# A hybrid decoder step whose first layer reads feature-major tokens and applies the norm to the sums

## The chip, the cores and the metric

The kernel runs on one core of a Trainium2 chip. The metric is device time in microseconds (us). The engines are PE (TensorE, matmuls and weight loads), DVE (VectorE), ACT (ScalarE), POOL (GpSimd) and SP (SyncE, which here issues nearly all DMAs). Each engine works through its own list of instructions in order, and semaphores tie the lists together.

## The reference

Two layers of a decoder run over 512 prompt tokens and 32 sample tokens of 1024 features. Cut to what matters:

```python
def _rmsnorm(x, w):
    return x * lax.rsqrt(jnp.mean(x * x, axis=-1, keepdims=True) + EPS) * w

h = _rmsnorm(x, norm_w)
z = h @ w_in                      # 1024 x 3584, split into ten parts
rq, rk, rv, rg, mq, mk, mv, mg, pu, pg = jnp.split(z, _split_points(), axis=-1)
# rq rk rv rg: retention; mq mk mv mg: block-sparse attention; pu pg: pooling
mq = _rope(_rmsnorm(_heads(mq), q_norm_w), pos)
mix = concat([r_o * silu(rg), m_o * silu(mg), p_o * silu(pg)])
y = x + mix @ w_out
```

Since 1/rms is one number per token, `h @ w_in` equals `((x * w) @ w_in) * (1/rms)`: the factor may be put on the sums.

## The kernel before

All matmuls of the projections are in fp32r with a split into a high and a low part: tokens and weights each become a rounded part and a remainder, and three products (high by high, low by high, high by low) are summed in PSUM. The split tokens lie in `XT`, feature-major (128 features in the partitions, 8 k-tiles, 544 tokens). The weights of a projection ("chunk") come in four slices of two k-tiles; `load_weights` issues their DMAs, `split_weights` has ACT write the high part into `whl` and DVE or POOL subtract for the low part. There are five `whl` buffers, four of which one chunk takes.

In layer 0 the tokens arrive token-major: `start` and `start2` load four tiles of 128 tokens, `rmsnorm` squares them on ACT, POOL takes the root, DVE multiplies by 1/rms and by the norm weights (spread over the partitions by two small matmuls in `spread_row`), PE transposes eight 128 x 128 blocks a tile, and ACT and DVE write the high and the low part into `XT`. Layer 1 does the same with the output of layer 0.

Then `dense` runs the chunks in the order mv, mq, mk, pu, pg, mg, rq, rv, rk, rg, o0, o1, o2. `tok_piece` takes a tile of 128 tokens against 384 (or 256) columns, 8 k-tiles by three products, 24 matmuls into one of two `acc` banks; `feat_piece` (pu and the gates) puts features in the partitions and 256 or 288 tokens in the columns. Sample tokens go through `sample_piece` into the bank `dec`, straight from the raw weights. After each piece a "post" task reads the bank: a copy (mv, rv), squares, rope and norm (`projected`: mq, mk), or tanh and two multiplications (`post_gate`).

The order on each engine is written out by a planner (`_Plan`). Tasks are generators that yield the engine wanted, the flags waited for and the buffers needed; the planner picks whichever can start first by its own table of costs, and for tasks that allow two engines (`ACT|DVE`, `DVE|POOL`, `ACT|POOL`) also the engine. What it picks is then fixed, and at run time every engine follows its list.

Of the kernel before, what the change touches and what calls it, by code (L numbers as in the profile page):

```python
# [18 lines left out]
D = 1024  # L19
# [273 lines left out]
def trunk(ctx, tc, depth, xp, xs, kv, sret, spool, pt, nrow, lpar, w384, w256, cst, y0,  # L293
# [93 lines left out]
    klz = const.tile([128, H, SEQ], F32R, name="klz")  # L387
    Sst = [const.tile([128, 3, 128], F32, name=f"Sst{i}") for i in range(2)]
# [17 lines left out]
    def raw_tag(ci, s_):  # L406
        return "pk" if ci == 0 and s_ > 1 else "wraw"
# [113 lines left out]
    def rmsnorm(l, t, L):  # L521
# [3 lines left out]
        if t == 4:  # L525
            yield R("SP", [("ys", l)], ["P", "P"])
            x = [buf("P")[:rows] for _ in range(2)]
            for half in range(2):
                S.dma_start(x[half], (xs if l == 0 else y0[SEQ:, :])[:, half * 512:half * 512 + 512])
                X.flag("xs", l, at=X.dma(64))  # L530
# [7 lines left out]
        else:  # L538
            x = ytile(t)
            first = l == 0 and t == 0  # L540
            pair = "xn", t // 2
            yield R("ACT", [("y", 0, 0, 0) if first else ("y", l, t)] + [("xn", l, t)] * (t % 2),
                    [] if t % 2 else [tag])
# [5 lines left out]
            if first:  # L549
                A.activation(xn3[:, 0:4], x[:, 0:4], AF.Square, accum_out=st[:, 0:1])  # L550
                yield R("ACT", [("y", 0, 0, 1)])
                A.activation(xn3[:, 4:8], x[:, 4:8], AF.Square, accum_out=st[:, 1:2])
                yield R("POOL")
                G.tensor_tensor(out=st[:, 0:1], in0=st[:, 0:1], in1=st[:, 1:2], op=OP.add)
            else:
                A.activation(xn3, x, AF.Square, accum_out=st[:, 0:1])
                yield R("POOL")
# [38 lines left out]
    def join_sample(a, out, W):  # L596

        half = W // 2
        yield R("ACT", (), ["t2"])
        t_ = buf("t2")  # L600
        A.copy(t_[:64, :half], a[64:128, :half])
        yield R("DVE")
        for m in range(2):
            rows = slice(NS * m, NS * m + NS)
            V.tensor_tensor(out=out[:, m * half:(m + 1) * half], in0=a[rows, :half], in1=t_[rows, :half], op=OP.add)
        X.put("t2")
        X.put("dec")

    def projected(a, dst, t, Ct, St, scale=None):
# [25 lines left out]
        if scale is None:  # L635
# [5 lines left out]
            rsq(st[:rows, 1, :H], st[:rows, 0, :H], H, rows, 1.0 / HD)  # L641
# [129 lines left out]
    def layer(l):  # L771
# [3 lines left out]
        def parameters():  # L775
            yield R("SP", (), ["pt"])
# [7 lines left out]
            else:  # L784
                S.dma_start(rowp[0:1, :D], nrow[l:l + 1, :D])
                X.flag("row1", at=X.dma(4))
                X.spawn(spread_row(), 0)
            X.flag("rowp issued", l)
            yield R("SP", [("cst1 issued",)])
# [4 lines left out]
            yield R("DVE", [("normed", l)])  # L794
            X.put("pt")

        def spread_row():

            yield R("POOL")
            ones = L["rowp"][0:1, D + 256:D + 384]  # L800
            G.memset(ones, 1.0)
            L["row"] = []
            for i, tag in enumerate(("pv", "dec")):
                yield R("PE", [("row1",)], [tag])
                a = ps(tag)
                mm(a, ones, L["rowp"][0:1, i * 512:(i + 1) * 512])
                L["row"].append(a)
                X.flag("row", l, i)
            X.spawn(warm(WARM), 0)
            yield R("DVE", [("normed", l)])  # L810
            X.put("pv")
            X.put("dec")
# [155 lines left out]
        def post_mq(t):  # L968
            def f(a):
                yield R("DVE", [("tabs", l, 0)], ["qk"])  # L970
                q_ = buf("qk")
                yield from projected(a, q_, t, L["tabs", 0][:, 0, t], L["tabs", 0][:, 1, t])
# [24 lines left out]

        def post_mv(t):
            def f(a):
                if t == 0:  # L1000
                    yield R("DVE", (), ["tv"])
                    L["tv"] = buf("tv").rearrange("p (t n) -> p t n", t=4)
                if t < 4:
                    yield R("ACT|DVE")
                    copy(L["tv"][:, t], a[:, :384])
                    X.put("acc")
                    X.flag("tv", l, t)
                    send(o_vp[l, t * 128:(t + 1) * 128], L["tv"][:, t], 196)
# [12 lines left out]
        def post_mk(t):  # L1021
            def f(a):
# [4 lines left out]
                yield from projected(a, k_, t, L["tabs", 1][:, 0, t], L["tabs", 1][:, 1, t])  # L1027
# [173 lines left out]
        def post_gate(k, half, sample_first, keys, done):  # L1201
# [4 lines left out]
            def f(a):  # L1206
                yield R("ACT", (), ["t1"])
# [17 lines left out]
        def post_rq(t):  # L1225
            def f(a):
# [3 lines left out]
                yield from projected(a, q_, t, cos[:, t], sin[:, t], False if t < 4 else rqs[:rows, t])  # L1230
# [13 lines left out]
        def post_rv(t):  # L1244
            def f(a):
# [3 lines left out]
                if t < 4:  # L1249
                    yield R("ACT|DVE")  # L1250
                    copy(L["rtv"][:, t], a[:, :384])
                    X.put("acc")
                    X.flag("rtv", l, t)
                else:
                    yield R("ACT", (), ["ks"])
                    vs = L["rvs"] = buf("ks")
                    yield from join_sample(a, vs[:NS], 384)
# [7 lines left out]
        def post_rk(t):  # L1265
            def f(a):
# [6 lines left out]
                yield from projected(a, k_, t, cos[:, t], sin[:, t], rks[:rows, t])  # L1273
# [54 lines left out]
        def ret_chunk(c):  # L1328
# [30 lines left out]
            yield from group_norm(on, H, reps[:, c])  # L1359
# [157 lines left out]
        def dense():  # L1517
# [7 lines left out]
            seen4 = [("x", l, 4, 0), ("x", l, 4, 1)]  # L1525
# [8 lines left out]
            yield from tokens("mv", post_mv, lambda t: [("x", l, t, 0), ("x", l, t, 1)])  # L1534
# [189 lines left out]
```

## Time and profile before

| | us |
|---|---|
| median of 3 runs | 717.33 |
| lowest, highest run | 715.79, 717.79 |
| the profiled execution | 717.02 |
| its span, first to last instruction | 715.3 |
| PE busy | 688.0 |
| DVE busy | 478.4 |
| ACT busy | 331.1 |
| POOL busy | 142.7 |

The span is 1.7 us shorter than the time of the same execution. Busy times are sums over the whole program and say little of a stage; for the stage that the change touches, the first 40 us, the rows further down give times from the span's start.

### The profile page before, as it was taken

What the parts mean: (1) busy time and instruction counts of PE and PEld (TensorE: products, weight loads), DVE (VectorE), ACT (ScalarE), POOL (GpSimd) and SP (SyncE); (2) the same over time, 40 slices, a digit from 0 to 9 for tenths busy, and PEclk for the clock granted to TensorE, in tenths of its full rate; (3) what the DMA queues carried; (4) which work ended last, traced back from release to release, by engine and by line L of the source; (5) the groups of instructions that cost most, each with busy time, mean ns of one, the idle gap of its engine ahead of it and who ended that gap; (6) DMA issues with size and microseconds to landing.
All of it is one profiled execution on the core that took longest, in us unless ns stands there. A gap on an engine that the chain in (4) does not pass through costs nothing.

```text
span 715.3 us, 16993 instructions
## 1 busy us (share of the span) xinstructions
PE 688.0 (96%) x5960; PEld 574.5 (80%) x5960; DVE 478.4 (67%) x1096; ACT 331.1 (46%) x844; POOL 142.7 (20%) x171
## 2 busy tenths in 40 slices
PE   7999989999999997989999999999999999999898
PEld 4888767777878796979989777777777878889798
DVE  4567888867554559786475688986845555887632
ACT  5535557663423413375164246776624234247511
POOL 5122422301001004342050223330101010035100
PEclk9999989999999999999999999999999999999999
DMA  9848888989999875005655679999999995020452
GB/s 282 262 129 254 283 259 277 291 272 315 303 329 309 255 286 167 21 2 185 216 149 173 199 257 324 286 309 298 293 298 322 316 317 178 23 76 2 161 179 77
DMA packets 113177, 159.76 MB, mean 223 GB/s; under 512 B 13763, under 2 KB 97860, under 8 KB 113093
## 3 DMA queue, kind: packets, MB, share of 16 engines
q1 hardware_dynamic: 112564, 158.43, 68.8%
q8 instruction: 47, 0.77, 0.4%
q14 instruction: 38, 0.30, 0.1%
q10 hardware_dynamic: 528, 0.26, 0.1%
HBM read 148.80 MB, written 9.84 MB: 222 GB/s over the span
## 4 chain that ended last, share of the span: by engine, by line
PE 83%; DVE 12%; issue 2%; ACT 2%; POOL 1%; DMA 1%; SPq 0%; DVEq 0%; POOLq 0%; ACTq 0%
PE acc L325 52%; PE dec L325 11%; PE pv L325 10%; PE tr L335 6%; PE att L325 3%; DVE t L287 2%; DVE whl L287 1%; DVE qk L287 1%; DVE mix L287 1%; DVE XT L287 1%; DMA pk<-kv 1%; DVE dP L287 1%; DVE P L287 1%; DVE kT L287 0%; DVE pv L287 0%
## 5 line engine op out<-in xcount | busy, mean ns | idle before, releaser
L325 PE MATMUL acc<-whl,XT 128*128 128x384 f32 (+1 forms) x1728 | 318.6, 337 | 2.4 <-DVE whl L287 1.7
L325 PEld LDWEIGHTS acc<-whl,XT 128*128 128x128 f32 x1728 | 287.6, 188 | 18.9 <-issue 13.1
L325 PE MATMUL acc<-XT,whl 128*128 128x256 f32 (+1 forms) x960 | 142.2, 299 | 1.1 <-DVE t L287 1.1
L325 PEld LDWEIGHTS acc<-XT,whl 128*128 128x128 f32 x960 | 127.3, 193 | 10.2 <-issue 8.1
L287 ACT CAST whl<-wraw 128x768 fp32r<-128x768 f32 (+1 forms) x102 | 79.1, 784 | 47.1 <-PE acc L325 32.3
L287 DVE TENSOR_TENSOR whl<-wraw,whl 128x768 fp32r<-128x768 f32 (+1 forms) x78 | 72.0, 931 | 33.5 <-ACT whl L287 31.9
L287 POOL TENSOR_TENSOR whl<-wraw,whl 128x768 fp32r<-128x768 f32 (+1 forms) x24 | 41.5, 1734 | 121.7 <-ACT whl L287 121.6
L325 PE MATMUL dec<-pk,qblk 128*32 128x256 f32 x768 | 50.9, 386 | 0.9 <-DMA pk<-kv 0.8
L325 PEld LDWEIGHTS dec<-pk,qblk 128*32 128x32 f32 x768 | 23.3, 110 | 19.7 <-issue 4.6
L287 DVE TENSOR_TENSOR pv<-pv,cst 128x384 f32<-128x384 f32 x40 | 22.5, 563 | 16.7 <-PE pv L325 16.5
L287 ACT ACTIVATE P<-att,ast 128x128 f32<-128x128 f32 (+3 forms) x48 | 25.2, 529 | 14.1 <-DVE ast L287 12.7
L287 DVE TENSOR_TENSOR mix<-acc,qk 128x384 f32<-128x384 f32 (+1 forms) x24 | 12.2, 509 | 24.9 <-PE acc L325 24.8
L287 POOL TENSOR_TENSOR qst<-qst,mhalf 128x6 f32<-128x6 f32 (+1 forms) x20 | 26.5, 1323 | 1.7
L287 POOL TENSOR_TENSOR mix<-mix,t 128x256 f32<-128x256 f32 x8 | 6.3, 789 | 102.6 <-DVE t L287 74.7
L287 ACT ACTIVATE dP<-dec,stat 128x256 f32<-128x256 f32 x32 | 15.2, 474 | 24.2 <-DVE stat L287 24.1
L287 DVE TENSOR_TENSOR t<-acc,cst 128x192 f32<-128x192 f32 (+1 forms) x48 | 17.3, 415 | 13.1 <-PE acc L325 13.1
L287 POOL TENSOR_SCALAR qst<-qst 128x6 f32<-128x6 f32 (+1 forms) x20 | 4.6, 230 | 102.1 <-DVE qst L287 98.9
L287 ACT ACTIVATE t<-acc 128x256 f32<-128x256 f32 (+1 forms) x32 | 12.6, 393 | 26.3 <-PE acc L325 24.4
L335 PE MATMUL tr<-cst,qk 128*128 128x128 f32 (+1 forms) x108 | 17.8, 273 | 4.3 <-DVE qk L287 3.8
L287 ACT COPY t<-dec 64x192 f32<-64x192 f32 (+1 forms) x18 | 5.6, 310 | 35.0 <-PE dec L325 34.8
L287 DVE TENSOR_REDUCE stat<-dec 128x1 f32<-128x256 f32 x32 | 13.5, 421 | 11.8 <-PE dec L325 11.4
L287 ACT ACTIVATE dPT<-dec 128x256 f32<-128x256 f32 x32 | 12.2, 381 | 19.6 <-PE pv L325 19.6
(469 smaller groups left out, 1210.3 us busy)
## 6 DMA issues: line engine op xcount, KB each, us to landing
pk<-kv SPq DMA_DIRECT2D x256, 192.0 KB, 3.8
wraw<-w SPq DMA_DIRECT2D x78, 384.0 KB, 4.7
wraw<-w SPq DMA_DIRECT2D x24, 256.0 KB, 4.4
y<-mix SPq DMA_DIRECT2D x4, 512.0 KB, 3.7
mix<-xp SPq DMA_DIRECT2D x3, 512.0 KB, 7.8
o_vp<-tv SPq DMA_DIRECT2D x8, 192.0 KB, 3.3
o_kp<-qk SPq DMA_DIRECT2D x8, 192.0 KB, 4.1
pt<-sret SPq DMA_DIRECT2D x2, 768.0 KB, 6.8
```

What stands on the lines that cost most here:

```text
L287: return f(*args, **kw)
L325: nc.tensor.matmul(out, lhsT, rhs, start=start, stop=stop)
L335: nc.tensor.transpose(out, in_, ident[:n, :n])
```

## The change

In layer 0 the tokens are now given in a feature-major layout (`xt`, two halves of 256 tokens by four pairs of k-tiles; `xst` for the samples), so nothing is transposed. `split_tokens` multiplies by the norm weights of the feature (`ncol`, one number per partition) while it splits: ACT or DVE writes the high part, DVE the low part. `norm_tokens` squares the tokens (`ACT|POOL`), adds the eight k-tiles (`DVE|POOL`), and a matmul with ones sums over the partitions; DVE and POOL make 1/rms per token, `rs`. `spread_norms` puts 1/rms of all tokens along the columns of `Rb` by matmuls of ones with a diagonal. The sums are then corrected: copies of mv and rv carry the scale (`scaled_copy`), the norms of mq and mk take a changed epsilon, pu and the gates are multiplied by `Rb` on DVE. The first chunk, mv, runs by k-tile pairs on two token tiles at once, first tokens 0 to 255 into the two `acc` banks, then 256 to 511 into the two `att` banks. Its raw weights lie in four `pk` buffers (two before), which the cached pages use later. Layer 1 is unchanged. The diff, cut to its core:

```diff
 def raw_tag(ci, s_):
-    return "pk" if ci == 0 and s_ > 1 else "wraw"
+    return "wraw" if ci else "pk"
...
+        def scaled_copy(out, a, t, keys=()):
+            if l:
+                yield R("ACT|DVE", keys)
+                copy(out(), a)
+                return
+            yield R("ACT|DVE", [("rs", t // 2), *keys])
+            if X.engine == "ACT":
+                A.activation(out(), a, AF.Copy, scale=rs[:, 1, t:t + 1])
+            else:
+                V.tensor_scalar(out(), a, rs[:, 1, t:t + 1], None, op0=OP.mult)
...
         def post_pu(f, half):
...
+                    yield R("DVE", [("U", l), ("Rb",)])
+                    V.tensor_tensor(out=L["U"][:, f, PBUF + n0:PBUF + n0 + 256], in0=a[:, :256],
+                                    in1=Rb[:, n0:n0 + 256], op=OP.mult)
...
         def post_gate(k, half, sample_first, keys, done):
...
+                if l == 0:
+                    yield R("DVE", [("Rb",)])
+                    V.tensor_tensor(out=a[:, :n], in0=a[:, :n], in1=Rb[:, n0:n1], op=OP.mult)
                 yield R("ACT", (), ["t1"])
                 th = buf("t1")
                 A.activation(th[:, :n], a[:, :n], AF.Tanh, scale=0.5)
...
-            yield from tokens("mv", post_mv, lambda t: [("x", l, t, 0), ("x", l, t, 1)])
+            if l:
+                yield from tokens("mv", post_mv, lambda t: [("x", l, t, 0), ("x", l, t, 1)])
+            else:
+                for h in range(2):
+                    for kp in range(4):
+                        yield R("PE", [("w", ci, kp), ("xk", h, kp)], [] if kp else ["att" if h else "acc"] * 2)
...
+                        for j in range(2):
+                            for k in (2 * kp, 2 * kp + 1):
+                                tok_piece(ci, "mv", 2 * h + j, a[j], KS_IN, k)
+                        if h:
+                            X.put("whl")
...
+    def split_tokens(h, kp):
+        cs = slice(256 * h, 256 * h + 256)
+        ks = (2 * kp, 2 * kp + 1)
+        yield R("ACT|DVE", [("xt", h, kp), ("ncol",)])
+        for k in ks:
+            if X.engine == "ACT":
+                A.activation(XT[:, k, 0, cs], mix[:, k, cs], AF.Copy, scale=ncolt[:, k:k + 1])
+            else:
+                V.tensor_scalar(XT[:, k, 0, cs], mix[:, k, cs], ncolt[:, k:k + 1], None, op0=OP.mult)
+        yield R("DVE")
+        for k in ks:
+            V.scalar_tensor_tensor(XT[:, k, 1, cs], mix[:, k, cs], ncolt[:, k:k + 1], XT[:, k, 0, cs].bitcast(F32),
+                                   op0=OP.mult, op1=OP.subtract)
+        X.flag("xk", h, kp)
+
+    def norm_tokens(h):
+        cs = slice(256 * h, 256 * h + 256)
+        tag = ("qT", "kT")[h]
+        for i in range(2):
+            yield R("ACT|POOL", [("xt", h, 2 * i), ("xt", h, 2 * i + 1)], [] if i else [tag])
...
+            if X.engine == "ACT":
+                A.activation(sq[:, 4 * i:4 * i + 4], x, AF.Square)
+            else:
+                G.tensor_tensor(out=sq[:, 4 * i:4 * i + 4], in0=x, in1=x, op=OP.mult)
+        yield R("DVE|POOL")
+        add2(sq[:, 0:4], sq[:, 0:4], sq[:, 4:8], OP.add)
+        yield R("DVE|POOL")
+        add2(sq[:, 0:2], sq[:, 0:2], sq[:, 2:4], OP.add)
+        yield R("DVE|POOL")
+        add2(sq[:, 0], sq[:, 0], sq[:, 1], OP.add)
+        yield R("PE", [("zeros",)], ["tr"])
+        p = ps("tr")
+        for j in range(2):
+            mm(p[:, j:j + 1], sq[:, 0, 128 * j:128 * j + 128], ones[:, 0:1])
...
+    def spread_norms():
...
+        for t in range(4):
+            A.mul(d_[:, t], ident, rs[:, 1, t:t + 1])
+        A.mul(ssum[:NS], ident[:NS, :NS], rs[:NS, 1, 4:5])
+        yield R("PE", (), ["tr", "tr"])
+        p, p4 = ps("tr"), ps("tr")
+        for t in range(4):
+            mm(p[:, t * 128:(t + 1) * 128], ones, d_[:, t])
+        X.put("P")
+        mm(p4[:, :NS], ones[:NS], ssum[:NS])
```

The program begins as follows on PE before the change. `tr<-cst,qT`, `tr<-cst,kT` are the transposes of prompt tokens, `acc<-whl,XT` the matmuls of mv, `pv<-pt` and `dec<-pt` the spreading of the norm weights, `att<-qblk` a matmul on zeros whose result nobody reads.

```order
L325 MATMUL att<-qblk 128x384
L325 MATMUL pv<-pt 128x512
L325 MATMUL dec<-pt 128x512
L325 MATMUL att<-qblk 128x384
L335 MATMUL tr<-cst,qT 128x128 x8
L325 MATMUL acc<-whl,XT 128x384 x18
L335 MATMUL tr<-cst,qT 128x128 x4
L325 MATMUL acc<-whl,XT 128x384 x6
L335 MATMUL tr<-cst,qT 128x128 x4
L335 MATMUL tr<-cst,kT 128x128 x4
L325 MATMUL acc<-whl,XT 128x384 x6
L335 MATMUL tr<-cst,kT 128x128 x4
```

After the change PE begins as follows; `tr<-ones,..` are the sums over the partitions, `tr<-P,ones` is the spreading of 1/rms, `dec<-wraw,X_71` is the sample piece of mq and `dec<-pk,X_71` that of mv.

```order
L325 MATMUL att<-qblk 128x384
L325 MATMUL acc<-whl,XT 128x384 x48
L325 MATMUL att<-whl,XT 128x384 x24
L325 MATMUL tr<-ones,qT 128x1 x2
L325 MATMUL att<-whl,XT 128x384 x12
L325 MATMUL tr<-ones,ssum 32x1 x4
L325 MATMUL tr<-ones,kT 128x1 x2
L325 MATMUL att<-whl,XT 128x384 x12
L325 MATMUL dec<-wraw,X_71 32x192 x16
L325 MATMUL acc<-whl,XT 128x384 x6
L325 MATMUL tr<-P,ones 128x128 x4
L325 MATMUL tr<-ssum,ones 128x32
```

The transposes are gone, the matmuls of mv stand at the head, and the small sums stand between its last pairs of k-tiles.

On POOL, behind the clearing of `klz` at the start, there stood before the roots of the first tile's norm and one low part of the weights:

```order
L287 MEMSET klz 64x3x512 x2
L287 MEMSET pt 1x128
L287 ISA
L287 TENSOR_TENSOR rst<-rst 128x1
L287 TENSOR_SCALAR rst<-rst 128x1
L287 TENSOR_TENSOR rst<-rst,mhalf 128x1
L287 TENSOR_TENSOR whl<-wraw,whl 128x768
```

Now there stand the squares of the first 256 tokens (`qT<-mix`), two of their additions (`qT<-qT`), and then the low part of mq's first slice:

```order
L287 MEMSET klz 64x3x512 x2
L287 ISA
L287 TENSOR_TENSOR qT<-mix 128x1024 x2
L287 TENSOR_TENSOR qT<-qT 128x1024
L287 TENSOR_TENSOR qT<-qT 128x512
L287 TENSOR_TENSOR whl<-wraw,whl 128x768
```

Four wide instructions have come to POOL that were not there. At the same time DVE, which began with the norm and the low parts of the first transposed tile, now has the low parts of the tokens (`XT<-mix,ncol,XT`) and all four low parts of mv's weights (`whl<-pk,whl`):

```order
L287 SCALAR_TENSOR_TENSOR XT<-mix,ncol,XT 128x256 x2
L287 TENSOR_TENSOR whl<-pk,whl 128x768 x2
L287 SCALAR_TENSOR_TENSOR XT<-mix,ncol,XT 128x256 x4
L287 TENSOR_TENSOR whl<-pk,whl 128x768 x2
L287 SCALAR_TENSOR_TENSOR XT<-mix,ncol,XT 128x256 x2
L287 TENSOR_SCALAR XT<-mix,ncol 128x256 x2
L287 SCALAR_TENSOR_TENSOR XT<-mix,ncol,XT 128x256 x8
L287 TENSOR_TENSOR X_71<-Rb,ncol 128x256
L287 TENSOR_TENSOR qT<-qT 128x256
```

Every one of the first nine wide steps reads two tensors from SBUF; before, the token steps read one of theirs from PSUM (the transposed block or the spread norm weights).

## Rows read from the trace of the kernel before

**Rows 1.** The page: busy time, share of the span and instructions.
```profile
PE 688.0 (96%) x5960; PEld 574.5 (80%) x5960; DVE 478.4 (67%) x1096; ACT 331.1 (46%) x844; POOL 142.7 (20%) x171
```

**Rows 2.** The page: the chain of waits that ended last, share by engine.
```profile
PE 83%; DVE 12%; issue 2%; ACT 2%; POOL 1%; DMA 1%; SPq 0%; DVEq 0%; POOLq 0%; ACTq 0%
```

**Rows 3.** PE in order of time: start, us, instructions, idle before and its releaser.
```profile
5.26 2.07 PE L325 MATMUL pv<-pt 1*128 1x512 f32 x2 [2.10 <-POOL pt L287]
...
12.15 0.44 PE L325 MATMUL acc<-whl,XT 128*128 128x384 f32 x1
12.87 3.24 PE L325 MATMUL acc<-whl,XT 128*128 128x384 f32 x17 [0.28 <-DVE XT L287]
...
30.33 7.65 PE L325 MATMUL acc<-whl,XT 128*128 128x384 f32 x42
37.91 1.51 PE L325 MATMUL dec<-wraw,X 128*32 128x192 f32 x32
39.35 8.68 PE L325 MATMUL acc<-whl,XT 128*128 128x384 f32 x48
...
115.86 1.02 PE L325 MATMUL dec<-tabs,par 128*128 128x512 f32 x2
```

**Rows 4.** Groups on PE, 0 to 38 us: busy, mean ns, idle before.
```profile
L325 PE MATMUL acc<-whl,XT 128*128 128x384 f32 x96 | 18.7, 345 | 0.3 <-DVE XT L287 0.3
...
L335 PE MATMUL tr<-cst,qT 128*128 128x128 f32 x16 | 3.0, 335 | 0.8 <-DVE qT L287 0.8
L335 PE MATMUL tr<-cst,kT 128*128 128x128 f32 x16 | 2.6, 283 | 1.1 <-DVE XT L287 1.1
```

**Rows 5.** SP's queue and ACT in order of time, from the start.
```profile
2.14 0.93 SPq L423 DMA_DIRECT2D wraw<-w  x2
...
3.44 0.63 ACT L287 ACTIVATE qT<-mix 128x512 f32<-128x512 f32 x1 [0.98 <-DMA mix<-xp]
...
6.37 0.83 ACT L287 CAST whl<-wraw 128x768 fp32r<-128x768 f32 x1 [1.34 <-DMA wraw<-w]
```

**Rows 6.** Stretches: PE, PEld, DVE, ACT, POOL busy, PEclk, DMA share, GB/s.
```profile
2.00:4.00 2.00, 1.17 (x2) 0.02 (x1) 0.00 (x0) 1.02 (x3) 1.89 (x3) 1.00 1.14 299
4.00:6.00 2.00, 0.74 (x1) 0.50 (x2) 0.00 (x0) 0.88 (x4) 1.77 (x5) 1.00 0.89 260
6.00:8.00 2.00, 2.00 (x4) 0.66 (x2) 0.44 (x1) 1.21 (x2) 1.12 (x2) 1.00 1.01 356
```

**Rows 7.** Groups on POOL, whole span.
```profile
L287 POOL TENSOR_TENSOR whl<-wraw,whl 128x768 fp32r<-128x768 f32 x19 | 34.9, 1837 | 115.8 <-ACT whl L287 115.8
...
L287 POOL TENSOR_TENSOR whl<-wraw,whl 128x512 fp32r<-128x512 f32 x5 | 6.7, 1342 | 5.9 <-ACT whl L287 5.7 <-DMA pk<-kv 0.2
```

**Rows 8.** Groups on DVE, whole span.
```profile
L287 DVE TENSOR_TENSOR att<-att,cst 128x256 f32<-128x256 f32 x24 | 10.2, 427 | 5.6 <-PE att L325 5.5
...
L287 DVE TENSOR_TENSOR whl<-pk,whl 128x768 fp32r<-128x768 f32 x2 | 1.9, 958 | 0.7 <-ACT whl L287 0.7
```

**Rows 9.** DVE in order of time, three places.
```profile
45.98 0.55 DVE L287 TENSOR_TENSOR qk<-t,qst 32x384 f32<-32x384 f32 x1
...
68.47 0.89 DVE L287 SCALAR_TENSOR_TENSOR tabs<-cst,pt 128x320 f32<-128x320 f32 x2
...
89.35 1.43 DVE L287 TENSOR_TENSOR ks<-t,qst 32x384 f32<-32x384 f32 x1
```

**Rows 10.** POOL in order of time, around the last of these.
```profile
87.55 2.82 POOL L287 TENSOR_TENSOR whl<-wraw,whl 128x512 fp32r<-128x512 f32 x2
```

**Rows 11.** Stretches, columns as in rows 6.
```profile
89.00:90.00 1.00, 0.00 (x0) 0.00 (x0) 0.90 (x2) 0.55 (x2) 1.00 (x1) 1.00 1.00 318
90.00:91.00 1.00, 0.07 (x1) 0.10 (x2) 0.97 (x2) 0.00 (x0) 0.37 (x1) 0.67 0.76 263
...
96.00:97.00 1.00, 1.00 (x13) 0.45 (x16) 0.37 (x2) 0.51 (x2) 0.00 (x0) 0.50 0.95 272
```

**Rows 12.** A group on PE, whole span: pieces of gates and pu, 256 tokens.
```profile
L325 PE MATMUL acc<-XT,whl 128*128 128x256 f32 x480 | 70.5, 297 | 0.7 <-DVE t L287 0.7
```

More of the change, by code (lines that the diff above doesn't have):

```diff
@@ L548, in rmsnorm @@
             xn3 = col3(xn)
[L549 to L557, printed above, removed]
+            A.activation(xn3, x, AF.Square, accum_out=st[:, 0:1])
+            yield R("POOL")
             x, xn = [x[:, 0:4], x[:, 4:8]], [xn[:, 0:512], xn[:, 512:D]]
@@ L793, in parameters @@
             yield from tables(1)
-            yield R("DVE", [("normed", l)])
+            yield R("DVE", [("normed", l)] if l else ())
             X.put("pt")
[L797 to L812, printed above, removed]
         def scales():
@@ L1002, in f @@
                     L["tv"] = buf("tv").rearrange("p (t n) -> p t n", t=4)
+                    X.flag("tvb", l)
                 if t < 4:
-                    yield R("ACT|DVE")
-                    copy(L["tv"][:, t], a[:, :384])
-                    X.put("acc")
+                    yield from scaled_copy(lambda: L["tv"][:, t], a[:, :384], t, [("tvb", l)])
+                    X.put("acc" if l or t < 2 else "att")
                     X.flag("tv", l, t)
@@ L1249, in f @@
                 if t < 4:
-                    yield R("ACT|DVE")
-                    copy(L["rtv"][:, t], a[:, :384])
+                    yield from scaled_copy(lambda: L["rtv"][:, t], a[:, :384], t)
                     X.put("acc")
@@ L1572, in begin @@
             X.spawn(scales(), 6)
[L1573 to L1574 removed]
+            if l:
+                for t in range(5):
+                    X.spawn(rmsnorm(l, t, L), 0)
         return {"dense": dense, "begin": begin, "L": L}
     def start():
[L1579 to L1584 removed]
@@ new lines, in split_sample @@
+    def split_sample():
+        x3 = Rb[:, :8 * NS].rearrange("p (k n) -> p k n", k=8)
+        cs = slice(SEQ, NTOK)
+        yield R("DVE", [("xst",), ("ncol",)])
+        V.tensor_tensor(out=X32, in0=x3, in1=ncolt[:, :, None].to_broadcast([128, 8, NS]), op=OP.mult)
+        yield R("ACT")
+        A.copy(XT[:, :, 0, cs], X32)
+        q3 = Rb[:, 8 * NS:16 * NS].rearrange("p (k n) -> p k n", k=8)
+        A.activation(q3, x3, AF.Square)
+        yield R("DVE")
+        V.tensor_tensor(out=XT[:, :, 1, cs], in0=X32, in1=XT[:, :, 0, cs].bitcast(F32), op=OP.subtract)
+        V.tensor_reduce(out=ssum, in_=q3.rearrange("p k n -> p n k"), axis=AX, op=OP.add)
+        X.flag("x", 0, 4, 0)
+        X.flag("x", 0, 4, 1)
+        yield R("PE", [("zeros",)], ["tr"], COLS32)
+        p = ps("tr")
+        for j in range(4):
+            mm(p[32 * j:32 * j + 32, 0:1], ssum, ones[:, 0:1])
+        yield R("DVE")
+        V.tensor_scalar(rs[:, 0, 4:5], p[:, 0:1], 1.0 / D, EPS, op0=OP.mult, op1=OP.add)
+        X.put("tr")
+        yield R("POOL")
+        G.tensor_tensor(out=rs[:, 1, 4:5], in0=rs[:, 0, 4:5], in1=mhalf[:, 0:1], op=OP.pow)
+        G.tensor_scalar(rs[:, 2, 4:5], rs[:, 0, 4:5], EPS, None, op0=OP.mult)
+        X.flag("rs", 2)
@@ new lines, in spread_norms @@
+    def spread_norms():
+        yield R("DVE", [("rs", 0), ("rs", 2), ("cst1",)])
+        for x, y, j in ((reps0, reps, 0), (rks0, rks[:, 0:4], 1)):
+            V.tensor_tensor(out=x, in0=y, in1=rs[:, j, 0:4, None].to_broadcast([128, 4, H]), op=OP.mult)
+        yield R("ACT", [("cst0",)], ["P"])
+        d_ = buf("P").rearrange("p (t n) -> p t n", t=4)
+        for t in range(4):
[7 more added lines that the diff above has]
+        mm(p4[:, :NS], ones[:NS], ssum[:NS])
+        yield R("ACT")
+        A.copy(Rb[:, :SEQ], p)
+        A.copy(Rb[:, SEQ:], p4[:, :NS])
+        X.put("tr", 2)
+        X.flag("Rb")
```

174 lines of the change are left out of this document (112 added, 62 removed).

## The prediction

> **What bounds the kernel now.** The page first: PE is busy for 688.0 us, 96% of the span [rows 1]; the chain of waits says the same from the other side, 83% PE and 12% DVE [rows 2]. So a microsecond that PE works less or idles less at the start comes off the end, unless PE waits for it later. Next the start, PE in order of time [rows 3]. The first matmul of mv runs at 12.15, the last of its 96 ends at 37.91, and the sample pieces of mv and mq have then 1.44 us of their own each (37.91 to 39.35 is the one of mq). 39.35, when the dense part of mq begins, is the mark by which I compare; without its two sample pieces mv is through at 36.47. In that stretch the 96 matmuls need 0.182 us each (42 in 7.65), 17.5 us. The rest of 12.15 to 36.47 is transposes, 3.0 and 2.6 us of them and more on samples, and 2.2 us of waits [rows 4].
>
> **What the change takes away.** All transposes, and the long road to the first matmul. Data bounds that road now: the first half tile of tokens, 256 KB, is waited for until 3.44, and the first weight slice, issued at 2.14 behind other transfers, until 6.37 [rows 5]. Afterwards 256 KB of tokens and that slice (393 KB) are the first in the queues. The rows on traffic give 0.60 MB by 4.0, 1.14 MB by 6.0 and 1.85 MB by 8.0 [rows 6], and 6.37 came about 0.85 us after the sum of what stood ahead (0.97 MB) had passed. So the slice lands at about 5.05, the pair of k-tiles behind the second slice (1.31 MB) at 7.3. A high part takes ACT 0.83 [rows 5], a low part DVE 0.96 [rows 8]: the low part of the first slice is there at 6.9, and PE starts its third product then instead of at 12.9. The table load of ACT now stands behind the arrival of the norm weights; it hides, since the slice lands later than both.
>
> **What the change adds at the start: POOL against DVE.** POOL gets three additions or products of 1024 columns and one of 512. From its rows, 1.34 us for 512 columns and 1.84 for 768 [rows 7], 1024 take 2.33, and the four take 8.3 us. DVE has, up to the low part of the third weight slice, two weight steps (0.96 each) and four token steps of 256 columns; two of 320 took 0.89 [rows 9], so I take 0.45 each: 3.7 us. Whether the two lie beside each other decides the forecast. The trace has the case: a DVE step of 32 x 384 with both inputs in SBUF takes 0.55 when POOL is idle; at 89.35 it took 1.43, and ended 0.41 after POOL's two wide subtractions (87.55 to 90.37) were over [rows 9, 10]. It did next to nothing until POOL had finished. All steps in question are of this sort. So the sum is serial: from 7.3, when POOL's first square and DVE's second weight step are both ready, 8.3 + 3.7 = 12.0, and the third weight slice has its low part at 19.3. The other end, side by side, is in the rivals. PE meanwhile does the first two pairs of k-tiles and waits.
>
> The Trainium skill states this as a rule (SBUF — State Buffer, "Who interferes with whom"): a VectorE instruction with two SBUF inputs and a GpSimd instruction that reads SBUF take one shared port, whoever is first holds it for the whole instruction, and the other is blocked. By that rule the sum stands as above, 716.6 in the end. Were the port shared out instead, DVE slowed to 1.43/0.55 = 2.6 times while POOL ran on, its 3.7 us would become 9.6 and the mark 2.4 us earlier, 714.2. The trace sides with the rule, by the 0.41 us.
>
> **From there to the mark.** From 19.3 PE has 10 matmuls of the third pair, 12 of the fourth and 48 of the second half, 70 x 0.182 = 12.7. Among them stand eight matmuls with ones. PE comes to those of tokens 256 to 511 before the last pair, and the sum they read is four steps back on DVE, behind the rope tables; I allow 1.2 us for the small matmuls and this wait. mv is through at 33.2, 3.3 us earlier than 36.47. What is late next is the spreading of 1/rms: POOL's last root waits for those same matmuls, ACT then builds the diagonals, and PE reaches the spreading after only six matmuls of mq. I take 0.9 us of waiting there and behind it, and 1.1 us for the four fp32 matmuls of 128 columns (a 512-column one is two instructions, 1.02 us at 115.86 [rows 3], so 0.26 each, and the rest is latency and the 32-column one). The bounds of this item are 1.1 (no wait) and 4 (a wait as long as the 2.1 us in front of the first spreading in before, and a little more). So 3.3 - 2.0 = 1.3 us remain.
>
> **The clock.** The granted clock reads 1.00 in the first stretches [rows 6], but the durations say 1.2 GHz: 512 columns from fp32 took 2.07 us at 5.26 and 1.02 at 115.86 [rows 3]. PE came to 2.4 GHz only by 12.87, after working almost without a break from 5.26. Half-rate matmuls before 19.3 cost nothing, as PE waits for data then anyway. Behind 19.3 a matmul of 384 columns takes 384/1200 = 0.32 us at 1.2 GHz instead of 0.182, so each microsecond at half rate costs 0.43. PE will have had gaps of about 2 us before, and a gap of 2 us at 89 was followed by a granted 0.50, 1.2 GHz, until 97 [rows 11]. I put 0.5 us here, bounds 0 and the 3.4 of the rival below.
>
> **The rest of layer 0.** Sixteen gate pieces get one more DVE step on PSUM, 0.43 each like `att<-att` [rows 8], and pu's copies move from ACT to DVE: 9 us of DVE in all, in a part where it has room. Each lies between a piece's last matmul and the release of its bank. The cover is the second bank: PE waited only 0.7 us in all in front of 480 matmuls of this kind [rows 12], and a piece of 24 takes over 3.4 us. If the cover were gone, 16 x (0.43 and a hop of 0.2) = 10 us. Of these ends I take 0.4, near the row. [...] The planner lays the rest out anew, by which I can forecast no sign; it widens the range by 2 us each way.
>
> **The sum.** The profiled execution took 717.02 (span 715.3 and 1.7 around it), 0.3 less than the median of 717.33. 717.0 - 3.3 + 2.0 + 0.5 + 0.4 = 716.6. Of this kernel 0.3%, 2.15 us, is what a measurement can tell, so this is no change: 715.2 to 719.5.
>
> **The rivals.**
> First, POOL and DVE do not hinder each other, or DVE gets ahead of POOL's squares and finishes the splits before them. For it: the weight steps are only four, and in the first 8 us data is scarce. Against it: the row at 89.35. Then PE starts at 6.95, has 17.5 us of matmuls, 1.7 more for about 4 us at half rate and 0.9 of small ones, and mv is through at 27.05, 9.4 earlier; less 2.0 and 0.4 it gives 717.0 - 7.0 = 710.0. Halfway, with DVE only slowed, it is some 714.
> Second, slower: the clock. A stop-and-go first half keeps PE at 1.2 GHz after 19.3. For it: seven microseconds passed before the clock rose in before, with PE busier than it will be now. Against it: from 19.3 PE is fed without a break. Seven further microseconds at half rate cost 7 x 0.43 = 3.0 us, or 3.4 with the half-empty microseconds around it, which gives 717.0 - 3.3 + 2.0 + 0.4 + 3.4 = 719.5 with the larger; with the whole second half at half rate 70 x 0.14 = 9.8, 726. If 2.4 GHz comes after 21.4, the 0.9 us that remain (1.3 less the gates' 0.4) are used up, and after 26.5 the loss can be measured. Between these ends I price it at 720.5.
> Third, slower: the gates. The extra step is queued behind the attention steps on DVE, whose waits for POOL at 83 to 90 the trace shows, and a bank comes free late. Against it: rows 12. At half of the 10 us, 721.5.
>
> **How the numbers follow.** The forecast has 0.48, of which 0.10 lies below 715.2, 0.35 between and 0.03 above 719.5. The first rival has 0.26, all faster. The clock has 0.19, 0.02 of it within 0.3%. The gates have 0.07. So faster 0.36, the same 0.37, slower 0.27. The likeliest one's own range is 714.0 to 719.5. To leave no more than 2 in 10 outside, the range reaches over half of the first rival and most of the clock: 709.5 to 721.5.
>
> **What would show it.** In the profile afterwards: POOL's squares from about 7 us, and DVE's `whl<-pk` and `XT<-mix` steps between 7 and 19 beginning late or lasting over 1.4 us; a wait of PE for DVE in the `acc` matmuls between 10 and 19; mv through at about 33; a wait in front of `tr<-P,ones`; and mq's dense part under way about 1 us earlier than now. If DVE's steps keep 0.45 and 0.96 us and PE runs through from 7, the first rival is right. If waits for DVE in front of the 256- and 288-column pieces grow from under 1 us to several, the third. What would make all of it wrong is a new long wait in layer 1, or a new order of the attention blocks that wins or loses several microseconds.

## The result and the profile after

The changed kernel takes 709.36 us (median of 4 runs, 708.43 to 710.07), the kernel before 717.56 (4 runs, 715.79 to 718.67): a ratio of 0.9887, 95% interval 0.9862 to 0.9912. That is 1.1% faster, where the forecast was no change (716.6, range 709.5 to 721.5): the time lies just below the range. The profiled execution took 708.43 with a span of 706.3, 9.0 us less than before.

The page, to set beside [rows 1, 2]: PE's busy time fell by 8.0 us and its idle time by 1.0, DVE's busy time rose by 13.

```profile
PE 680.0 (96%) x5940; PEld 572.4 (81%) x5940; DVE 491.5 (70%) x1130; ACT 331.4 (47%) x839; POOL 147.4 (21%) x165
...
PE 79%; DVE 12%; ACT 2%; issue 2%; DMA 2%; POOL 1%; SPq 1%; DVEq 0%; POOLq 0%; ACTq 0%
```

PE in order of time at the start, to set beside [rows 3]:

```profile
6.21 6.98 PE L325 MATMUL acc<-whl,XT 128*128 128x384 f32 x26 [3.04 <-ACT whl L287]
13.86 2.18 PE L325 MATMUL acc<-whl,XT 128*128 128x384 f32 x11 [0.67 <-DVE whl L287]
18.34 2.20 PE L325 MATMUL acc<-whl,XT 128*128 128x384 f32 x11 [2.30 <-DVE XT L287]
20.38 4.38 PE L325 MATMUL att<-whl,XT 128*128 128x384 f32 x24
...
28.57 2.35 PE L325 MATMUL att<-whl,XT 128*128 128x384 f32 x12
30.85 1.51 PE L325 MATMUL dec<-wraw,X 128*32 128x192 f32 x32
32.29 1.31 PE L325 MATMUL acc<-whl,XT 128*128 128x384 f32 x6
33.44 1.15 PE L325 MATMUL tr<-P,ones 128*128 128x128 f32 x8
34.51 0.40 PE L325 MATMUL tr<-ssum,ones 32*128 32x32 f32 x2
35.70 1.51 PE L325 MATMUL dec<-pk,X 128*32 128x192 f32 x32 [0.78 <-DVE qk L287]
37.14 5.54 PE L325 MATMUL acc<-whl,XT 128*128 128x384 f32 x30
```

The mark, mq's dense part behind both sample pieces, is now at 37.14, with six of mq's matmuls (1.1 us) already done: it answers to 39.35 + 1.1 = 40.45 of before. The start gained 3.3 us in this execution. The two restarts at 13.86 and 18.34 wait for DVE. These are DVE's and then POOL's rows in that stretch:

```profile
11.16 2.64 DVE L287 TENSOR_TENSOR whl<-pk,whl 128x768 fp32r<-128x768 f32 x1
13.73 3.16 DVE L287 TENSOR_TENSOR whl<-pk,whl 128x768 fp32r<-128x768 f32 x1
16.81 1.87 DVE L287 SCALAR_TENSOR_TENSOR XT<-mix,ncol,XT 128x256 fp32r<-128x256 f32 x2
```

```profile
7.07 2.70 POOL L287 TENSOR_TENSOR qT<-mix 128x1024 f32<-128x1024 f32 x1 [1.85 <-DMA mix<-xt]
11.09 1.90 POOL L287 TENSOR_TENSOR qT<-mix 128x1024 f32<-128x1024 f32 x1 [1.32 <-DMA mix<-xt]
13.07 3.00 POOL L287 TENSOR_TENSOR qT<-qT 128x1024 f32<-128x1024 f32 x1
...
16.14 1.86 POOL L287 TENSOR_TENSOR qT<-qT 128x512 f32<-128x512 f32 x1
```

DVE's rows are the low parts of the third and the fourth weight slice and two token steps. Read both lists by their ends: POOL's square ends at 12.99, DVE's third weight step 0.8 later, POOL's addition at 16.07, DVE's fourth weight step at 16.89, POOL's last addition at 18.00, the first of DVE's token steps 0.3 later, and PE restarts at 18.34. The engines take turns, and nothing is gained by overlap. This is the rule of the Trainium skill that the prediction weighed (SBUF — State Buffer, "Who interferes with whom"), and the rows agree: the two weight steps take 5.73 together (11.16 to 16.89) where one alone took 0.96 [rows 8].

5.7 of the 9.0 us came behind the mark. Two stretches hold nearly all of it: PE's busy time, count, granted clock, DMA share and GB/s, first of before, then of after:

```profile
72.00:108.00 36.00, 32.36 (x309) 0.91 0.86 267
252.00:324.00 72.00, 65.61 (x588) 0.98 0.34 114
```

```profile
72.00:108.00 36.00, 33.48 (x316) 0.95 0.86 278
252.00:324.00 72.00, 68.47 (x626) 0.98 0.47 153
```

In the first, PE idles 1.1 us less and the clock gives back some 0.04 x 36 = 1.4; in the second it idles 2.9 less: 5.4 together. After the change the granted clock stood at 0.50 from within the first to within the last of the following stretches (columns as in [rows 6]), some 3.4 us where it was 6.8 [rows 11]:

```profile
89.00:90.00 1.00, 1.00 (x8) 1.00 (x7) 0.97 (x4) 0.30 (x2) 1.00 (x2) 0.56 1.01 299
...
92.00:93.00 1.00, 1.00 (x8) 0.98 (x7) 0.97 (x5) 0.58 (x3) 0.00 (x0) 0.74 1.04 317
```

### The profile page after: what moved, and what is told of

The parts are those of the page before. It is cut to its first block, busy times and chain, and to the rows that moved or that the text cites. A ratio compares the mean times of both kernels' runs of the same rounds, so it can differ in the third digit from the quotient of the medians.

```text
span 706.3 us, 16977 instructions
## 1 busy us (share of the span) xinstructions
PE 680.0 (96%) x5940; PEld 572.4 (81%) x5940; DVE 491.5 (70%) x1130; ACT 331.4 (47%) x839; POOL 147.4 (21%) x165
## 4 chain that ended last, share of the span: by engine, by line
PE 79%; DVE 12%; ACT 2%; issue 2%; DMA 2%; POOL 1%; SPq 1%; DVEq 0%; POOLq 0%; ACTq 0%
PE acc L325 50%; PE dec L325 10%; PE pv L325 10%; PE tr L335 6%; PE att L325 3%; DVE whl L287 2%; DVE qk L287 2%; DVE t L287 1%; DVE XT L287 1%; DMA wraw<-w 1%; DMA mix<-xt 1%; DVE mix L287 1%; SPq L1638 1%; ACT whl L287 1%; DVE pt L287 1%
## 5 line engine op out<-in xcount | busy, mean ns | idle before, releaser
L325 PE MATMUL acc<-whl,XT 128*128 128x384 f32 (+1 forms) x1680 | 313.2, 339 | 8.2 <-ACT whl L287 3.0
L325 PEld LDWEIGHTS acc<-whl,XT 128*128 128x128 f32 x1680 | 282.6, 190 | 26.1 <-issue 12.5
L325 PE MATMUL acc<-XT,whl 128*128 128x256 f32 (+1 forms) x960 | 139.5, 296 | 1.0 <-DVE t L287 1.0
L325 PEld LDWEIGHTS acc<-XT,whl 128*128 128x128 f32 x960 | 125.0, 190 | 8.8 <-issue 6.3
L287 ACT CAST whl<-wraw 128x768 fp32r<-128x768 f32 (+1 forms) x100 | 76.9, 781 | 40.7 <-PE acc L325 30.2
L287 DVE TENSOR_TENSOR whl<-wraw,whl 128x768 fp32r<-128x768 f32 (+1 forms) x79 | 74.1, 947 | 28.8 <-ACT whl L287 27.5
L287 POOL TENSOR_TENSOR whl<-wraw,whl 128x768 fp32r<-128x768 f32 (+1 forms) x21 | 36.8, 1752 | 123.3 <-ACT whl L287 123.3
L287 DVE TENSOR_TENSOR mix<-acc,qk 128x384 f32<-128x384 f32 (+1 forms) x24 | 12.2, 509 | 22.5 <-PE acc L325 22.1
L287 ACT COPY PT<-tr 128x128 f32<-128x128 f32 (+3 forms) x41 | 16.4, 422 | 17.3 <-PE tr L335 17.2
L287 ACT ACTIVATE dPT<-dec 128x256 f32<-128x256 f32 x32 | 12.2, 381 | 21.1 <-PE pv L325 21.1
L335 PE MATMUL tr<-cst,P 128*128 128x128 f32 x120 | 20.0, 281 | 1.5 <-DVE P L287 0.7
```

Source lines behind the costliest of these rows:

```text
L287: return f(*args, **kw)
L325: nc.tensor.matmul(out, lhsT, rhs, start=start, stop=stop)
L335: nc.tensor.transpose(out, in_, ident[:n, :n])
```

## The experiments

**What is gained behind the mark: the change or its layout?** The changed start shifts every later decision of the planner. To see what a new layout alone does, one cost in its table was moved by 0.01 or 0.02 us, in either kernel. The work stays the same, the first rows of every engine stand, and the rest comes in another order.

```diff
-    HOP = {"PE": 0.2, "ACT": 0.2, "DVE": 0.18, "POOL": 0.2, "SP": 0.12}
+    HOP = {"PE": 0.2, "ACT": 0.2, "DVE": 0.19, "POOL": 0.2, "SP": 0.12}
```

Expected of before with 0.19, then with 0.17:

> The kernel before, with one cost in the planner's table raised by 0.01 us (the hop of DVE); the work, the buffers and the order of the first 38 to 48 rows on PE, DVE and ACT are those of before, and everything behind them is laid out anew. Theory A, the gain of the change behind its 37th microsecond (5.7 of the 9.0 us that the span lost) is an outcome of a new layout as such: this kernel differs from before by several microseconds in either direction, with the mark at the start unmoved; scatter of 2 to 5 us. Theory B, that gain comes from the change itself (its operations, freed buffers, the earlier start): this kernel stays within 1.5 us of before, 716 to 719.

> As the run with the hop raised, here lowered by 0.01 us: a second new layout of the same work. Theory A: 2 to 5 us off before, and off the first one, with the start unmoved. Theory B: 716 to 719.

Of the changed kernel with 0.19, then with 0.17:

> The changed kernel with the hop of DVE raised by 0.01 us in the planner's table; the first 42 rows or more on each engine unchanged, the rest laid out anew. Theory A: the time scatters by 2 to 5 us around a value nearer to 709.4 + 3 than to 709.4, since 709.4 was a lucky layout; 708 to 716. Theory B: within 1.5 us of the changed kernel, 708 to 711.

> As the run above, with the hop lowered by 0.01 us; here the first 86 rows or more are unchanged. Theory A: 708 to 716. Theory B: 708 to 711.

Then 0.20 and 0.16, of before and of the changed kernel:

> The kernel before with the hop of DVE in the planner's table at 0.20 in place of 0.18: a fourth layout of the same work, with the start in place. Theory A, behind the start the time is a matter of the layout: anywhere from 712 to 721, the mean of the layouts of before staying near 716.6. Theory B, the change brings 5 us behind the start: the layouts of before stay above 714 all.

> The kernel before with the hop at 0.16, a fifth layout. Theory A: 712 to 721. Theory B: above 714.

> The changed kernel with the hop at 0.20, a fourth layout. Theory A, it differs from before by the 3.3 us of the start and the scatter of layouts: anywhere from 709 to 720, the mean of the layouts near 713.3. Theory B, the change itself brings 9: 707 to 712, and the 719.6 was the odd one.

> The changed kernel with the hop at 0.16, a fifth layout. Theory A: 709 to 720, mean of the layouts near 713.3. Theory B: 707 to 712.

Measured, medians in us; the ratio to before in the same set of runs has its interval behind it:

| hop | before | after |
|---|---|---|
| 0.16 | 712.14, 0.9939 [0.9916, 0.9962] | 714.05, 0.9951 [0.9925, 0.9978] |
| 0.17 | 717.56, 0.9993 [0.9975, 1.0012] | 713.11, 0.9927 [0.9910, 0.9943] |
| 0.18 (as given) | 717.56 | 709.36, 0.9887 [0.9862, 0.9912] |
| 0.19 | 714.55, 0.9951 [0.9934, 0.9967] | 719.55, 1.0018 [1.0000, 1.0037] |
| 0.20 | 721.76, 1.0064 [1.0041, 1.0087] | 715.43, 0.9973 [0.9946, 1.0000] |
| mean, standard deviation | 716.7, 3.6 | 714.3, 3.7 |

The row with 0.18 has the 4 runs of the result; larger sets put before at 717.0 to 718.1. The mark, mq's dense part behind both sample pieces, stands at 39.25 to 39.37 in all five layouts of before and at 37.03 to 38.20 in those of after (38.20 is that with 0.20, where twelve of mq's matmuls are done by then in place of six): the start is the change's own. Behind it the same work scatters over some 10 us. The means differ by 2.4 us with a standard error of 2.3 (3.65 times the root of 2/5); that fits the 3.1 us between the mean marks, both with six of mq's matmuls done (40.4 and 37.3). With so few layouts, up to 7.7 us would still be within the 95% interval, so a further gain of up to 4.6 from the change is not excluded, but nothing asks for one: 709.36 is the lowest of its five.

Theory A fits and theory B does not: all four new layouts of after lie above B's 711 or 712, and before with 0.16 lies under its 714. Single ranges missed all the same. Before with 0.17 did not move, as B had it, and A's ranges were too narrow at the top for after with 0.19 (719.55, where they ended at 716) and before with 0.20 (721.76, where they ended at 721). The same two stretches, in the layouts with 0.19, of before and then of after:

```profile
72.00:108.00 36.00, 34.65 (x329) 1.00 0.91 298
252.00:324.00 72.00, 67.10 (x599) 0.98 0.39 125
```

```profile
72.00:108.00 36.00, 31.64 (x276) 0.81 0.75 241
252.00:324.00 72.00, 66.74 (x624) 1.00 0.44 145
```

The kernel before also reaches a full clock at 72 to 108, and the changed one can have it far worse: 1.8 us more idle time and 0.14 x 36 = 5.0 us of clock than in the layout given, 6.9 of the 12.2 us between these spans. Elsewhere other places lose: before with 0.20 idles only 1.7 and 2.6 us in these two stretches, at a full clock, and loses 6.3 us of PE's time here:

```profile
432.00:468.00 36.00, 29.69 (x288) 0.95 0.85 270
```

**What makes PE wait at 90 us?** The prediction's row for the port, `ks<-t,qst` held up by POOL [rows 9, 10], stands right before PE's longest wait of that stretch. Low parts of pu's and pg's weights were put on DVE where the planner had put them on POOL, in before (three) and in the slowest layout of after, that with 0.19 (four). The planner is charged as if nothing had changed, so all else keeps its place; the same device serves in all runs below.

```diff
+                    if l == 0 and n in ("pu", "pg") and X.engine == "POOL":
+                        nc.vector.tensor_tensor(out=hl[:, 1, :W2], in0=raws[ci, s_][:, :W2], in1=hl[:, 0, :W2].bitcast(F32),
+                                                op=OP.subtract)
+                        X.use("POOL", 0.153 + W2 * 0.0021)
```

> The kernel before, with three low parts of pu's and pg's weights (128 x 512) put on DVE where the planner put them on POOL; the planner charges what it charged before, so every other row on every engine stands where it stood. Theory A: the wait of 2.12 us in front of the transposes of ks at 88.8 to 90.9 comes from POOL's two subtractions holding up a small DVE step, and the granted clock of 0.50 from 90.3 to 97.1 from that gap. Then the wait falls under 0.6 us, the clock reads 1.00 there, and the time falls by 2 (the wait) to 4.6 us (with 5.7 busy microseconds at half rate): 713 to 715.5. Rival: the chain of DVE steps is late by itself, or the clock falls for another reason; then the time stays within 1 us of before.

> The changed kernel in the slow layout (hop of DVE raised by 0.01, 719.6 us), with four low parts of pu's and pg's weights put on DVE in place of POOL and nothing else moved. Theory A: the wait of 1.92 us before the transposes of ks (85.4 to 87.3) and the clock of 0.50 from 87.0 to 100.7 are gone; 1.9 and up to 5 us, so 712.5 to 715. Rival: 718 to 720, the slow layout is slow for other reasons.

Measured: 717.40 (0.9996 [0.9978, 1.0014]) and 719.13 against 719.55 (1.0015 [0.9983, 1.0046] of before). No gain: a miss for theory A. PE in before, then in before so changed, then the clock of the latter:

```profile
90.93 0.49 PE L335 MATMUL tr<-cst,ks 32*128 32x32 f32 x3 [2.12 <-DVE ks L287]
...
93.02 2.93 PE L325 MATMUL acc<-XT,whl 128*128 128x256 f32 x12 [0.72 <-DVE t L287]
```

```profile
90.07 0.34 PE L335 MATMUL tr<-cst,ks 32*128 32x32 f32 x3 [1.45 <-DVE ks L287]
90.74 0.40 PE L325 MATMUL dec<-kTs,qblk 128*32 128x32 f32 x24 [0.33 <-ACT kTs L287]
92.76 2.60 PE L325 MATMUL acc<-XT,whl 128*128 128x256 f32 x12 [1.63 <-DVE t L287]
```

```profile
92.00:93.00 1.00, 0.24 (x2) 1.00 1.04 192
93.00:94.00 1.00, 1.00 (x7) 0.59 0.59 137
94.00:95.00 1.00, 1.00 (x7) 0.50 0.92 353
```

The wait for `ks` shrank from 2.12 to 1.45 us, and the next one, 0.72 before, grew to 1.63. The clock fell all the same, for a shorter time (about 3.5 us). DVE has no gap of note from 83 to 93 in either kernel, and its step `t<-acc`, for which PE waits last, ended at 92.97 in before and at 92.70 now: the three subtractions took on DVE nearly all of the time that POOL's hold-up had cost it. That fits a chain of DVE steps that is too long at that place; with the subtractions left out altogether it was not tried. (The profiled execution of this kernel took 714.0, its ten runs 714.0 to 719.3: a span of one execution is no verdict here.)

**What does the port cost at the start, and does a microsecond there reach the end?** POOL's four wide steps, and with them the last small addition on DVE, were left out; then they were kept but moved, the squares to ACT and the additions to DVE.

```diff
             else:
-                G.tensor_tensor(out=sq[:, 4 * i:4 * i + 4], in0=x, in1=x, op=OP.mult)
+                X.use("POOL", 0.153 + 1024 * 0.0021)
...
-            mm(p[:, j:j + 1], sq[:, 0, 128 * j:128 * j + 128], ones[:, 0:1])
+            mm(p[:, j:j + 1], sq[:, 0, 128 * j:128 * j + 128] if h else ones, ones[:, 0:1])
```

> The changed kernel without POOL's four wide steps at the start (squares of tokens 0 to 255 and two of their additions) and the last addition on DVE: the norms of these tokens are left out, the matmul with ones reads ones instead. The planner charges for them as before, so all other rows keep their places. Theory A, POOL's steps hold DVE's up on the shared port: DVE's third and fourth weight step take 1.0 us each in place of 5.7 together, mv is through at 27.0 to 28.0 in place of 30.85, and mq's dense part begins 2.5 to 3.5 us earlier. Theory B, the data bounds the start: mv through after 30. For the end: if a microsecond at the start is a microsecond at the end, 706 to 707; if it is absorbed, 708.5 to 709.5.

Measured: 704.72 (0.9816 [0.9780, 0.9851]), 4.6 us under the changed kernel. PE, and DVE's groups (busy, mean ns, idle before):

```profile
6.22 11.67 PE L325 MATMUL acc<-whl,XT 128*128 128x384 f32 x48 [3.05 <-ACT whl L287]
17.73 4.38 PE L325 MATMUL att<-whl,XT 128*128 128x384 f32 x24
...
27.52 1.51 PE L325 MATMUL dec<-wraw,X 128*32 128x192 f32 x32
...
32.99 5.18 PE L325 MATMUL acc<-whl,XT 128*128 128x384 f32 x28
```

```profile
L287 DVE SCALAR_TENSOR_TENSOR XT<-mix,ncol,XT 128x256 fp32r<-128x256 f32 x16 | 6.7, 479 | 5.1 <-ACT XT L287 5.1
L287 DVE TENSOR_TENSOR whl<-pk,whl 128x768 fp32r<-128x768 f32 x4 | 3.7, 956 | 0.3 <-ACT whl L287 0.2
```

The second group in the changed kernel:

```profile
L287 DVE TENSOR_TENSOR whl<-pk,whl 128x768 fp32r<-128x768 f32 x4 | 7.6, 1927 | 0.2 <-ACT whl L287 0.2
```

The first had 638 ns there. Without POOL the weight step takes 956, PE runs through, mv is through at 27.52, and the mark moves by 4.15 us. The end moves by about as much. Theory A on both counts, and further than it said (2.5 to 3.5 at the mark, 706 to 707 at the end). As work was left out too, the move below is the cleaner test of the port.

The steps kept, but off POOL:

```diff
             if X.engine == "ACT":
+                if i == 0:
+                    while late_squares:
+                        nc.scalar.activation(*late_squares.pop(0), AF.Square)
                 A.activation(sq[:, 4 * i:4 * i + 4], x, AF.Square)
             else:
-                G.tensor_tensor(out=sq[:, 4 * i:4 * i + 4], in0=x, in1=x, op=OP.mult)
+                late_squares.append((sq[:, 4 * i:4 * i + 4], x))
+                X.use("POOL", 0.153 + 1024 * 0.0021)
```

> The changed kernel with the four wide steps taken off POOL and kept: the squares of tokens 0 to 255 stand on ACT ahead of the squares of tokens 256 to 511, their two wide additions on DVE ahead of the third; every other row keeps its place. Theory A, the port: DVE's splits run at their free durations, mv is through at 27.5 to 28.5, mq's dense part begins at 33 to 34 in place of 37.1, and since a microsecond at the start is one at the end, 705 to 706.5. Rival: the additions (2.3 us on DVE) and the squares (2.1 us on ACT) delay the splits of tokens 256 to 511 instead, mv through after 30, 708 to 710.

> The same move in the slow layout of the changed kernel (hop of DVE raised by 0.01, 719.6 us), all other rows of that layout in place. Theory A, the gain at the start and the layout behind it add up: 3 to 4.5 us off 719.6, 715 to 716.5. Rival, an earlier start meets other waits in this layout: any time within 2 us of 719.6.

> The same move in the third layout of the changed kernel (hop of DVE lowered by 0.01, 713.1 us). Theory A: 3 to 5 us off, 708 to 710. Rival: within 2 us of 713.1.

Measured: 706.75 (0.9847 [0.9819, 0.9876]), the lowest of any kernel here that does all the work; 716.47 (0.9982 [0.9958, 1.0005]); 711.33 (0.9896 [0.9863, 0.9929]). PE in the first:

```profile
6.18 10.83 PE L325 MATMUL acc<-whl,XT 128*128 128x384 f32 x48 [3.01 <-ACT whl L287]
16.84 4.38 PE L325 MATMUL att<-whl,XT 128*128 128x384 f32 x24
21.78 0.58 PE L325 MATMUL tr<-ones,qT 128*128 128x1 f32 x4 [0.56 <-DVE qT L287]
...
28.32 1.51 PE L325 MATMUL dec<-wraw,X 128*32 128x192 f32 x32
...
34.70 5.54 PE L325 MATMUL acc<-whl,XT 128*128 128x384 f32 x30
```

The marks move by 2.4, 2.3 (37.22 to 34.92) and 3.0 us (37.99 to 35.01), the medians by 2.6, 3.1 and 1.8: the same on average, 2.6 and 2.5. The mark fell short of the 3 to 4 us expected, since the sums now come late from DVE (0.56 and 0.85 us of waits in the first layout). So a microsecond at the start is about one at the end, on average over three layouts; singly the medians are too coarse to tell. The third is a miss for theory A: 1.8 lies under its 3 to 5 and within the rival's 2, though the times of its four runs span 4.6 us.

**What is the order by k-tiles worth?** Tokens 0 to 255 of mv token tile by token tile again:

```diff
-                                tok_piece(ci, "mv", 2 * h + j, a[j], KS_IN, k)
+                                if j == 0 or h:
+                                    tok_piece(ci, "mv", 2 * h + j, a[j], KS_IN, k)
+                                else:
+                                    X.use("PE", 3 * (n / 2400 + 0.013))
+                                    stage.append(k)
+                        if kp == 3:
+                            for k in stage:
+                                tok_piece(ci, "mv", 2 * h + 1, a[1], KS_IN, k)
```

> The changed kernel with the matmuls of tokens 0 to 255 of mv in the old order, token tile by token tile, in place of pairs of k-tiles on two token tiles; the planner charges the same, and nothing else moves. It tells what that part of the change is worth. Theory A, PE waits for the splits at the start, and the order by k-tiles gives it work in the meantime: by 18.3 it has done 18 matmuls in place of 37, so mv is through 19 x 0.182 = 3.5 us later, at 34.3, and the time is 3 to 3.5 us longer, 712 to 713. Rival, the work behind the wait runs at the full clock either way and the wait moves elsewhere: less than 1 us.

Measured: 713.48 (0.9949 [0.9926, 0.9973]), 4.1 us over the changed kernel.

```profile
10.75 2.61 PE L325 MATMUL acc<-whl,XT 128*128 128x384 f32 x7 [0.93 <-DVE XT L287]
16.60 1.97 PE L325 MATMUL acc<-whl,XT 128*128 128x384 f32 x5 [3.24 <-DVE whl L287]
18.94 6.50 PE L325 MATMUL acc<-whl,XT 128*128 128x384 f32 x29 [0.37 <-DVE XT L287]
...
40.53 5.53 PE L325 MATMUL acc<-whl,XT 128*128 128x384 f32 x30
```

The waits are as long, but less stands between them. The mark, 40.53, is that of before (40.45). In this execution DVE's first token step began 0.6 us later than in that of the changed kernel (5.71 against 5.07), which no edit explains, so of the 3.4 us between their marks some 2.8 are the order's. With the splits as they are, the order by k-tiles is thus most of the start's gain of 3.3; the earlier data, the missing transposes and the new sums nearly cancel. The time lost, 4.1, is a little more than the 3 to 3.5 expected.

**What do the gates' extra steps cost?** The 16 multiplications were left out:

```diff
-                    V.tensor_tensor(out=a[:, :n], in0=a[:, :n], in1=Rb[:, n0:n1], op=OP.mult)
+                    X.use("DVE", (n + 66) / 960.0)
```

> The changed kernel without the 16 multiplications by 1/rms in front of the gates of layer 0 (left out: the gates' sums aren't scaled), all other rows in place. Theory A, the second bank covers them: 0 to 0.5 us faster, 708.9 to 709.4. Rival, they lie on the path of the banks: 16 x 0.6 = up to 10 us faster, under 706.

Measured: 708.87 (0.9887 [0.9845, 0.9929]), 0.5 us under the changed kernel, which is within the noise. That excludes the rival's 10 us and fits theory A; the changed kernel itself shows 1.0 us of waits before these pieces, where [rows 12] had 0.7:

```profile
L325 PE MATMUL acc<-XT,whl 128*128 128x256 f32 x480 | 68.7, 291 | 1.0 <-DVE t L287 1.0
```

**The port has no fixed order.** The run without the gates' multiplications has the start of the changed kernel, instruction for instruction, and yet its profile shows another start. DVE's second weight step, then PE and its clock:

```profile
7.24 2.65 DVE L287 TENSOR_TENSOR whl<-pk,whl 128x768 fp32r<-128x768 f32 x1
```

```profile
17.24 5.66 PE L325 MATMUL acc<-whl,XT 128*128 128x384 f32 x22 [3.38 <-DVE whl L287]
...
37.98 5.54 PE L325 MATMUL acc<-whl,XT 128*128 128x384 f32 x30
```

```profile
19.00:20.00 1.00, 1.00 (x4) 1.00 (x4) 1.00 (x4) 0.00 (x0) 0.00 (x0) 0.50 1.07 393
```

Here POOL's first square, begun at 7.11, came ahead of DVE's second weight step; in the changed kernel that step began at 7.07 and came first. PE then waits 3.38 us in one piece instead of 0.67 and 2.30, the granted clock stands at 0.50 from 18.8 to 22.1, the 22 matmuls take 0.26 us each, and the mark comes at 37.98, 0.84 later. The profile with 0.17 shows a like wait (3.73 us) and a mark of 37.99. So a mark read from one execution is uncertain by about a microsecond wherever two engines race for the port, the 3.3 us of gain included, and part of the 3.0 us by which the mark moved with 0.17 is this race.

## Why the prediction was wrong, point by point

**The layout term failed, and it is most of the 7.2 us.** "The planner lays the rest out anew, by which I can forecast no sign; it widens the range by 2 us each way." No sign was right. The size was not: five layouts of each kernel scatter with a standard deviation of 3.6 us, so the difference of two layouts has one of 5. The layout given happened to be 4.9 us under the mean of its five, which is luck as far as the runs tell. The mean, 714.3, would have been the forecast to make for this change, with a range of some 8 us each way, about twice that scatter. The trace of before had the sign of it: a wait of 2 us at 90, with a granted clock of 0.50 for 6.8 us behind it, is a thing that a new order can halve (3.4 us in the layout given) or double (13.7 us in that with 0.19).

**The start: right mechanism, wrong size.** "The third weight slice has its low part at 19.3" and "mv is through at 33.2" were 13.8 and 30.85. POOL and DVE do exclude each other, as the 12.0 us of the serial sum assumed, but the sum had two things wrong. It put all four of POOL's steps in front of the third weight step. The engines took turns instead, so that only the two squares stood in front of it; the two additions held up the fourth weight step and the tokens behind it. And the sum began with the second weight step, which was done by 8.0, before POOL's square could hold it up: 389 GB/s came in between 4 and 6 us where before had 260 [rows 6], so that the second slice followed right behind the first (ACT splits both without a pause from 5.34). So 59 matmuls were left at 18.34 in place of 70 at 19.3: 11 x 0.182 + 1.0 = 3.0 us better, less 0.6 for the small matmuls and their waits (12.5 us from 18.34 to 30.85 less 59 x 0.182 leaves 1.8, where 1.2 was allowed). The start gained 3.3 where 1.3 was forecast.

**The spreading of 1/rms** (2.0): 37.14 - 30.85 less the two sample pieces (1.44 each) and the six matmuls (1.15) leaves 2.3. Right.

**The clock** (0.5, and the second rival): 24 matmuls in 4.38 from 20.38 are 0.182 each, the full rate, and the 11 before them took 0.20. The term was nearly zero in this execution. What the rival describes does happen: with the other order at the port the clock stood at 0.50 from 18.8 to 22.1, and 22 matmuls took 5.66 us where they need 4.0. That cost 1.7 us and not 3.4, and the rival's slower kernel did not come. The length of the gap alone does not decide it: 2.30 us in front of 18.34 left the clock at 1.00 here, while in the profile with 0.16 a wait of 1.73 in front of 17.62 was followed by 0.50.

**The gates** (0.4, and the third rival): 0.5, within the noise of that run. The waits of PE in front of the pieces, 0.7 us before and 1.0 after, bear the term out; the rival is wrong. The scaled copies of mv and rv, for which the sum has no term, took ACT 0.58 us each where plain ones take 0.48 in the same profile; no run shows what that is worth.

**The first rival**, POOL and DVE without hindrance, had mv through at 27.05 and 710.0. The time came out near it, but by another way: POOL hindered DVE all the same, and it cost 3.3 us until mv was through, as the run without POOL's steps shows (27.52 for 30.85, which also bears out the rival's own 27.05). A time that agrees with a rival does not make the rival right.

## What to carry to other kernels

Where a planner writes the order, time a change in several layouts (a cost moved by 0.01 us was enough here) before saying what it brings, or charge the planner the old cost and keep the order fixed; then effects of 2 to 4 us could be told here in spite of a scatter of 10. Read a change at the start by a mark in the trace, in more than one execution: a microsecond at the mark was about one at the end. While data is still arriving, order the first matmuls by what has arrived, and keep wide GpSimd steps off the stretch in which VectorE prepares it.

## What the hardware showed unexpectedly

With both queues full, two engines that exclude each other took strict turns, instruction by instruction, in both directions: POOL's addition of 1024 columns lasted 3.00 us with 0.7 of a DVE step at its head, as DVE's subtraction lasted 3.16 behind it and 0.96 without it. Which of them went first differed between executions with the same lists.

One kernel's own runs spread with the granted clock. The ten runs of the changed kernel with 0.16 took 711.8 and 712.3 us where the mean granted clock was 0.998, and 716.7 where it was 0.983 and 0.986.
